# One hybrid decoder block: the memory attention split into three steps that overlap between units, and its second score matmul on all 128 rows

## The chip, the cores and the metric

The kernel runs on one core of a Trainium2 chip. The metric is the time of one execution in device microseconds; lower is better. The engines are TensorE (PE for its matmuls, PEld for its weight loads), VectorE (DVE), ScalarE (ACT), GpSimd (POOL) and SyncE (SP, which here only issues DMAs).

## What is computed

One decoder layer over 1024 tokens of width 1024: a norm, one wide input projection, three mixers (a gated delta rule, a stick-breaking attention, a cross-attention into 256 memory tokens), gates, an output projection and a final norm. The change touches the third mixer alone:

```python
def memory_attention(q, mk, mv):
    s = jnp.einsum('bhtd,bhmd->bhtm', q, mk).astype(jnp.float32) * (1.0 / math.sqrt(q.shape[-1]))
    p = jax.nn.softmax(s, axis=-1)
    return jnp.einsum('bhtm,bhmd->bhtd', p.astype(mv.dtype), mv)
```

There are 4 heads of width 64; q has 1024 rows, mk and mv have 256.

## The kernel before

Operands of matmuls are kept as two parts, high and low (h and l), and a product is three matmuls, high by high, high by low, low by high (helper `mm3`, L160 to L162). The helper `split` makes the parts: ScalarE writes the high part (L143), VectorE the low one (L144).

The input projection is a stream of jobs (`stream`), each of 7 slots of 12 matmuls of 512 columns on TensorE (tiles mmX, mmY, mmZ). Each slot has its weights loaded by SP (L153, tiles wb), subtracted (L203) and split (tiles wu), and its results taken out of PSUM by ScalarE (L230, L247) and VectorE. The PSUM bank of mmZ has one buffer, so a new group of mmZ waits until ScalarE has read the last one at L247.

Beside this stream run generators, which are called between slots in step with the progress of the stream: the triangular solver (VectorE, L648 and L651), then `memory()`, then `combine()` (L717 on: pairs of DMA loads into tiles with one buffer, 64x64 matmuls Y and X, and a store). `memory()` is spread over 32 slots that begin after the job of its queries, `mq`, which stores them to DRAM in parts (mqs_d); these slots belong to the jobs dz and mz.

In `memory()` a unit is one head and 256 rows of q (two blocks of 128). There are 16 units, 4 for each head. The tile q holds a head's high part in rows 0 to 63 and its low part in rows 64 to 127. The tile k holds the high part of k in both halves of its first plane, and the low part in the upper half of its second plane. For each block of a unit the score is two matmuls into the same PSUM tile ms: L683 contracts all 128 rows, L684 contracts 64 rows (high q by low k). Then come the row maximum (L687, L688), the exponential with its sum (L692), the reciprocal (L694), the scaling (L696), four transposes into PSUM tile mT (L700) and a split into pTh and pTl. After two units the value product runs, 6 matmuls into tile mo, and is copied out (L712) and stored (L713). Tiles ms, mo, Y and X share two PSUM banks (tag wk); mT has the tag tr with two.

The program's order is not the order in which the engines run. A planner takes the instructions in the program's order as priorities, simulates them with durations of its own, and writes a fixed list for each engine; so each engine then runs its list in order and waits where something is late.

Of the kernel before, what the change touches and what calls it, by code (L numbers as in the profile page):

```python
# [11 lines left out]
F32 = mybir.dt.float32  # L12
F32R = mybir.dt.float32r
AF = mybir.ActivationFunctionType
ALU = mybir.AluOpType
AX = mybir.AxisListType
# [3 lines left out]
P = 128  # L20
T = 1024
NT = 8
# [15 lines left out]
def hybrid_block(ctx, tc, x, mem, norm_g, mem_norm_g, wq, wv0, wba, convw, a_log, dt_bias,  # L38
                 dn_g, wmk, wmv, wbd, wbs, wbm, wout, final_g, out):
    nc = tc.nc  # L40
    ve, sc, gp, pe, sy = nc.vector, nc.scalar, nc.gpsimd, nc.tensor, nc.sync

    def pool(name, bufs, space=None, side="left", stack=ctx):
        kw = dict(name=name, bufs=bufs, reuse_waits="tile")
        if space is None:
            kw["side"] = side
        else:
            kw["space"] = space
            if space == DRAM:
                kw.pop("reuse_waits")  # L50
        return stack.enter_context(tc.tile_pool(**kw))
# [21 lines left out]
    def psum(tag, name):  # L73
        if tag == "X" and "X" not in banks["tags"]:
            tag = "z"
        if tag in MM:
            return mmp.tile([P, 512], F32, tag=tag, bufs=MM[tag], name=name)
        return banks["pool"].tile([P, 512], F32, tag=tag, bufs=banks["tags"][tag], name=name)
# [4 lines left out]
    ident = cst.tile([P, P], F32, name="ident")  # L83
# [19 lines left out]
    def dscr(name, shape, dt=F32):  # L103
        return dr.tile(shape, dt, name=name)
# [16 lines left out]
    om_d = dscr("om_d", [2, P, T])  # L121
# [3 lines left out]
    mk_d = dscr("mk_d", [2, 2, P, 256])  # L125
    mv_d = dscr("mv_d", [2, P, 2, 256])
    mqs_d = dscr("mqs_d", [2, 4, 64, T])
# [11 lines left out]
    def f(ap):  # L139
        return ap.bitcast(F32)  # L140

    def split(dst, src, on=ve):
        sc.activation(dst[0], src, AF.Copy)  # L143
        on.tensor_tensor(out=dst[1], in0=src, in1=f(dst[0]), op=ALU.subtract)  # L144
# [11 lines left out]
    def mm3(o, pairs, first=True, again=False):  # L156

        n, kw = len(pairs), dict(skip_group_check=True) if again else {}
        for i, (ah, al, bh, bl) in enumerate(pairs):
            pe.matmul(o, ah, bh, start=(first and i == 0), stop=False, **kw)  # L160
            pe.matmul(o, ah, bl, start=False, stop=False, **kw)  # L161
            pe.matmul(o, al, bh, start=False, stop=(i == n - 1), **kw)  # L162
# [89 lines left out]
    def half(i):  # L252
        return slice(i * 512, i * 512 + 512)
# [14 lines left out]
    def row(src, tb):  # L268
        t = ap_.tile([P, T], F32, tag="xt", bufs=4, name=f"xt_{tb}")
        sy.dma_start(out=t, in_=src[0, tb * P:tb * P + P, :])  # L270
        return t
# [92 lines left out]
    rows_ = {tb: row(x, tb) for tb in (0, 4)}  # L364
# [38 lines left out]
    def staged(nm):  # L403
        return st.tile([P, 512], F32, tag="st", bufs=3, name=nm)
# [258 lines left out]
    def memory():  # L663
        mv = [mp_.tile([P, 2, 256], F32R, name=f"mv{j}") for j in "hl"]
        for j in range(2):
            sy.dma_start(out=f(mv[j]), in_=mv_d[j])
        for h in range(4):
            i, r0 = h // 2, (h % 2) * 64

            q = mp_.tile([P, T], F32R, tag="q", bufs=2, name=f"q_{h}")  # L670
            k = mp_.tile([P, 2, 256], F32R, tag="k", bufs=2, name=f"k_{h}")
            for j in range(2):
                sy.dma_start(out=f(q[j * 64:j * 64 + 64]), in_=mqs_d[j, h])
                sy.dma_start(out=f(k[j * 64:j * 64 + 64, 0, :]), in_=mk_d[0, i, r0:r0 + 64])
            sy.dma_start(out=f(k[0:64, 1, :]), in_=mk_d[1, i, r0:r0 + 64])
            for tb in range(0, NT, 2):
                c0 = tb % 4 * P
                if c0 == 0:
                    pT = [mp_.tile([P, 2, 512], F32R, tag=f"pT{j}", name=f"pT{j}_{h}_{tb}") for j in "hl"]
                s = psum("wk", f"ms_{h}_{tb}")  # L680
                for j in range(2):
                    ts = slice((tb + j) * P, (tb + j) * P + P)
                    pe.matmul(s[:, j * 256:(j + 1) * 256], q[:, ts], k[:, 0, :], start=True, stop=False)  # L683
                    pe.matmul(s[:, j * 256:(j + 1) * 256], q[0:64, ts], k[0:64, 1, :], start=False, stop=True)  # L684
                sv = s.rearrange("p (a b) -> p a b", a=2)
                mx = mp_.tile([P, 2], F32, tag="mx", bufs=2, name=f"mx_{h}_{tb}")
                ve.tensor_reduce(out=mx, in_=sv, axis=AX.X, op=ALU.max)  # L687
                ve.tensor_scalar(out=mx, in0=mx, scalar1=-0.125, scalar2=None, op0=ALU.mult)  # L688
                pt = mp_.tile([P, 2, 256], F32, tag="pt", bufs=2, name=f"pt_{h}_{tb}")
                sm = mp_.tile([P, 2], F32, tag="sm", bufs=2, name=f"sm_{h}_{tb}")  # L690
                for j in range(2):
                    sc.activation(pt[:, j, :], sv[:, j, :], AF.Exp, bias=mx[:, j:j + 1], scale=0.125,  # L692
                                  accum_out=sm[:, j:j + 1])
                ve.reciprocal(out=sm, in_=sm)  # L694
                for j in range(2):
                    sc.activation(pt[:, j, :], pt[:, j, :], AF.Copy, scale=sm[:, j:j + 1])  # L696
                o = psum("tr", f"mT_{h}_{tb}")
                for c in range(2):
                    for j in range(2):
                        pe.transpose(o[:, (c * 2 + j) * P:(c * 2 + j + 1) * P], pt[:, j, c * P:(c + 1) * P], ident)  # L700
                split([t[:, :, c0:c0 + 256] for t in pT], o.rearrange("p (a b) -> p a b", a=2))
                yield
                if c0 == 0:
                    continue
                hf = tb // 4
                mo = psum("wk", f"mo_{h}_{hf}")

                hs = slice(i * P, i * P + P)
                mm3(mo, [(mv[0][:, c, hs], mv[1][:, c, hs], pT[0][:, c, :], pT[1][:, c, :])
                                        for c in range(2)])  # L710
                t = staged(f"mot_{h}_{hf}")
                sc.activation(t[r0:r0 + 64], mo[r0:r0 + 64], AF.Copy, scale=0.5)  # L712
                sc.dma_start(out=om_d[i, r0:r0 + 64, half(hf)], in_=t[r0:r0 + 64])  # L713
                yield

    def combine():
# [100 lines left out]
                split([t[:, g * 4:g * 4 + 4, n * P:n * P + P] for t in odn], zt)  # L817
                yield

    SOLVE, MEM, COMB, RECUR = 1 + 1 + 62 + 8, 4 * 6, 16, 1 + 16 * 4  # L820

    def pacer(gen, total):
        done = [0]
# [21 lines left out]
    qk = {}  # L845
# [69 lines left out]
    for c in (15, 13, 11, 9, 7, 5, 3):  # L915
# [5 lines left out]
                            op0=ALU.mult, op1=ALU.mult)  # L921
# [36 lines left out]
    mp_ = pool("M", 1, stack=m_st)  # L958
    while pos[1] <= mark["v"]:
        slot()  # L960
        beside()
    mem_ = pacer(memory(), MEM)
    comb = pacer(combine(), COMB)
    start2 = pos[0]
# [22 lines left out]
    def weights(h, i):  # L987

        w = (i + 1) * P
        t = qk[h]  # L990
        pf = dp.tile([P, T + 1], F32, tag="pf", bufs=2, name=f"pf_{h}_{i}")
        gp.memset(pf[:, T:T + 1], 1.0)  # L992
        off = T - w
        halves = [(0, w)] if w <= 512 else [(w // 2, w), (0, w // 2)]
        ts_ = slice(i * P, i * P + P)
        for c0, c1 in halves:
            o = psum("z", f"z_{h}_{i}_{c0}")[:, 0:c1 - c0]
            mm3(o, [(t["qh"][:, ts_], t["ql"][:, ts_], t["kh"][:, c0:c1], t["kl"][:, c0:c1])])
            be = dp.tile([P, 512], F32, tag="be", bufs=2, name=f"be_{h}_{i}_{c0}")[:, 0:c1 - c0]
            pv = pf[:, off + c0:off + c1]  # L1000
            sc.activation(pv, o, AF.Sigmoid, scale=-SBS)  # L1001
            sc.activation(be, o, AF.Sigmoid, scale=SBS)  # L1002
            if c1 == w:
                for d, fl in ((pf[:, T - P:T], 1.0), (be[:, c1 - c0 - P:c1 - c0], 0.0)):
                    gp.affine_select(out=d, in_=d, compare_op=ALU.is_gt, fill=fl, base=0,  # L1005
                                     pattern=[[-1, P]], channel_multiplier=1)
            ve.tensor_tensor_scan(out=pv[:, ::-1], data0=pv[:, ::-1], data1=pv[:, ::-1],  # L1007
                                  initial=pf[:, off + c1:off + c1 + 1], op0=ALU.mult, op1=ALU.bypass)
            d = pf[:, off + c0 + 1:off + c1 + 1]
            ve.tensor_tensor(out=d, in0=be, in1=d, op=ALU.mult)  # L1010
        return pf[:, off + 1:T + 1]
# [175 lines left out]
    for tb in range(NT):  # L1187
# [11 lines left out]
        for k, hf in order:  # L1199
            s = half(hf)  # L1200
# [5 lines left out]
        for hf in range(2):  # L1206
            s = half(hf)
# [6 lines left out]
        for hf in range(2):  # L1214
            s = half(hf)
# [79 lines left out]
```

## Time and profile before

| | |
|---|---|
| median of 3 runs | 1628.51 us (1625.81 to 1630.97) |
| the profiled execution, own time | 1621.97 us |
| its span, first to last instruction | 1620.3 us |
| TensorE busy | 1549.0 us, 96% |
| VectorE, ScalarE, GpSimd busy | 1180.3, 819.6, 312.5 us |
| mean granted TensorE clock | 0.986 |

The stage in which `memory()` runs lies from about 599 to 782 us of the span. A matmul's duration in the profile is longer than the time it takes up, since matmuls overlap: the distance from one start to the next is what a stream of them costs.

### The profile page before, as it was taken

The page shows a single profiled execution, that of the slowest core. Times are in us where ns is not written, and L with a number is a line of the kernel's source. Part 1 is how long each engine was busy: PE and PEld are TensorE (multiplying, and loading weights), DVE is VectorE, ACT ScalarE, POOL GpSimd, SP SyncE. Part 2 cuts the span into 40 slices and gives each one's busy share as a digit, 9 for nine tenths or more (in the row PEclk, how much of TensorE's full clock was granted, in tenths as well). Part 3 has the DMA queues.
Part 4 walks back from the last instruction along what each step waited for, and adds up shares of the span by engine and source line. Part 5 has one row for each costly group of instructions (what it writes and reads, how often), then busy time and mean ns, then how long its engine had stood idle before and what let it go on. Part 6 is the DMA issues. An engine that isn't in the chain of part 4 may idle for free.

```text
span 1620.3 us, 23277 instructions
## 1 busy us (share of the span) xinstructions
PE 1549.0 (96%) x7979; PEld 1299.1 (80%) x7979; DVE 1180.3 (73%) x1903; ACT 819.6 (51%) x1909; POOL 312.5 (19%) x567
## 2 busy tenths in 40 slices
PE   6899999999999998998999999999998999979998
PEld 6888888887888776776788888888886888868786
DVE  8688989879999997553587778878867755544333
ACT  7578877765555435544455545545554322232121
POOL 4516445331113200000011111111110110110011
PEclk9999999999999998998999999999999999999999
DMA  8337556563333465233322322332138966644232
GB/s 290 97 106 222 160 154 195 164 201 100 109 104 118 143 195 168 83 111 86 119 78 92 103 79 90 107 105 79 66 124 255 304 195 181 206 126 133 82 104 78
DMA packets 152359, 223.32 MB, mean 138 GB/s; under 512 B 39984, under 2 KB 68144, under 8 KB 151984
## 3 DMA queue, kind: packets, MB, share of 16 engines
q1 hardware_dynamic: 107424, 159.94, 32.7%
q10 hardware_dynamic: 35712, 32.51, 6.1%
q0 software_dynamic: 9104, 29.37, 5.4%
q8 instruction: 63, 1.03, 0.3%
q14 instruction: 56, 0.46, 0.1%
HBM read 150.36 MB, written 71.40 MB: 137 GB/s over the span
## 4 chain that ended last, share of the span: by engine, by line
PE 83%; DVE 6%; DMA 5%; ACT 3%; issue 2%; SPq 0%; POOL 0%; ACTq 0%; DVEq 0%; POOLq 0%
PE mmY_g L160 3%; PE mmY_g L162 3%; PE mmY_g L161 3%; PE mmY_skq L160 2%; PE aTp L1033 2%; PE mmY_skq L161 2%; PE mmY_skq L162 2%; PE out L1203 2%; PE out L1201 2%; PE out L1202 2%; PE y_ydn L1135 2%; PE y_ydn L1136 2%; PE y_ydn L1137 2%; PE y_ysb L1136 2%; PE y_ysb L1135 2%
## 5 line engine op out<-in xcount | busy, mean ns | idle before, releaser
L1007 DVE TENSOR_TENSOR_SCAN pf<-pf 128x512 f32<-128x512 f32 (+4 forms) x96 | 97.1, 1012 | 15.7 <-POOL pf L1005 15.7
L143 ACT ACTIVATE aTh<-aTp 128x512 fp32r<-128x512 f32 (+2 forms) x96 | 44.6, 497 | 62.8 <-PE aTp L1033 59.5
L144 DVE TENSOR_TENSOR aTl<-aTp,aTh 128x512 fp32r<-128x512 f32 (+2 forms) x96 | 50.5, 546 | 25.7 <-ACT aTh L143 25.7
L992 POOL MEMSET pf<- 128x1 f32 x64 | 6.0, 98 | 327.0 <-PE aTp L1033 181.0
L1005 POOL TENSOR_SCALAR_AFFINE_SELECT pf<-pf 128x128 f32<-128x128 f32 x64 | 26.5, 415 | 204.7 <-ACT pf L1001 204.7
L1001 ACT ACTIVATE pf<-z 128x512 f32<-128x512 f32 (+4 forms) x96 | 47.1, 498 | 28.6 <-PE z L162 24.9
L1010 DVE TENSOR_TENSOR pf<-be,pf 128x512 f32<-128x512 f32 (+4 forms) x96 | 53.4, 557 | 3.7
L651 DVE TENSOR_TENSOR M<-M,tmp 128x62 f32<-128x62 f32 (+30 forms) x62 | 53.5, 863 | 0.3
L648 DVE TENSOR_TENSOR tmp<-M 128x62 f32<-128x62 f32 (+30 forms) x62 | 53.2, 858 | 0.2
L1201 PE MATMUL out<-oh_wo,mh 128*128 128x512 f32 x128 | 50.0, 391 | 1.5 <-ACT mh L143 1.5
L1135 PE MATMUL y_ydn<-odnh,w_ydn 128*128 128x512 f32 x128 | 49.5, 391 | 1.7 <-ACT odnh L143 1.7
L1049 PE MATMUL av<-aTl,vh 128*128 128x256 f32 (+1 forms) x160 | 47.0, 294 | 3.8 <-DVE aTl L144 3.7
L1135 PE MATMUL y_ysb<-oh_sb,w_ysb 128*128 128x512 f32 x128 | 50.6, 395 | 0.0
L1137 PE MATMUL y_ysb<-oh_sb,w_ysb 128*128 128x512 f32 x128 | 50.5, 395 | 0.0
L1136 PE MATMUL y_ysb<-ol_sb,w_ysb 128*128 128x512 f32 x128 | 50.3, 393 | 0.0
L1137 PE MATMUL y_ydn<-odnh,w_ydn 128*128 128x512 f32 x128 | 49.9, 390 | 0.0
L1136 PE MATMUL y_ydn<-odnl,w_ydn 128*128 128x512 f32 x128 | 49.8, 389 | 0.0
L1202 PE MATMUL out<-ol_wo,mh 128*128 128x512 f32 x128 | 49.8, 389 | 0.0
L1002 ACT ACTIVATE be<-z 128x512 f32<-128x512 f32 (+4 forms) x96 | 47.3, 503 | 4.2 <-DVE pf L1010 4.0
L1203 PE MATMUL out<-oh_wo,ml 128*128 128x512 f32 x128 | 49.3, 389 | 0.0
L1048 PE MATMUL av<-aTh,vh 128*128 128x256 f32 (+1 forms) x160 | 45.2, 283 | 1.4 <-ACT aTh L143 1.4
L1208 DVE TENSOR_TENSOR xo<-out,xo 128x512 f32<-128x512 f32 x16 | 11.0, 691 | 48.0 <-PE out L1203 48.0
(818 smaller groups left out, 5535.4 us busy)
## 6 DMA issues: line engine op xcount, KB each, us to landing
wb_g_b<-in_wq_dram SPq DMA_DIRECT2D x48, 256.0 KB, 2.8
wb_kq_b<-in_wq_dram SPq DMA_DIRECT2D x32, 256.0 KB, 3.0
wb_skq_b<-in_wq_dram SPq DMA_DIRECT2D x32, 256.0 KB, 2.7
g_d<-g ACTq DMA_DIRECT2D x32, 256.0 KB, 2.0
xt<-in_x_dram SPq DMA_DIRECT2D x8, 512.0 KB, 4.6
wb_sz_b<-in_wq_dram SPq DMA_DIRECT2D x16, 256.0 KB, 3.6
kt_d<-kq ACTq DMA_DIRECT2D x16, 256.0 KB, 3.4
gam<-gr_d SPq DMA_DIRECT2D x8, 512.0 KB, 4.4
```

What stands on the lines that cost most here:

```text
L160: pe.matmul(o, ah, bh, start=(first and i == 0), stop=False, **kw)
L161: pe.matmul(o, ah, bl, start=False, stop=False, **kw)
L162: pe.matmul(o, al, bh, start=False, stop=(i == n - 1), **kw)
L651: ve.tensor_tensor(out=d, in0=d, in1=t, op=ALU.add)
L1007: ve.tensor_tensor_scan(out=pv[:, ::-1], data0=pv[:, ::-1], data1=pv[:, ::-1], initial=pf[:, off + c1:off + c1 + 1], op0=ALU.mult, op1=ALU ...
L1010: ve.tensor_tensor(out=d, in0=be, in1=d, op=ALU.mult)
L1135: pe.matmul(oo[hf], wh, oh[:, s], start=(k == 0), stop=False)
L1136: pe.matmul(oo[hf], wh, ol[:, s], start=False, stop=False)
L1137: pe.matmul(oo[hf], wl, oh[:, s], start=False, stop=(k == n - 1))
L1201: pe.matmul(oo[hf], mh[:, k, :], wo[k][0][:, s], start=(k == 0), stop=False)
L1202: pe.matmul(oo[hf], mh[:, k, :], wo[k][1][:, s], start=False, stop=False)
L1203: pe.matmul(oo[hf], ml[:, k, :], wo[k][0][:, s], start=False, stop=(k == KC - 1))
```

## The change

The loop over heads and blocks is cut into four functions. `operands(h)` loads q and k of a head; `scores(n)` does unit n up to its scaled weights; `weights(n)` does its transposes and split; `values(p)` does the value product of units 2p and 2p+1 and its store. They are issued so that `scores(n)` stands ahead of `weights(n-1)` and `values(p)` stands behind `scores(2p+3)`; operands of the next head are issued at the second unit of a head. The k tile now holds the high part of k in both halves of the first plane and the low part in both halves of the second, so that both score matmuls contract 128 rows (high and low q by high k, high and low q by low k). A head's k is loaded with two DMAs of both planes in place of three of one plane. The number of steps over which the pacing spreads the generator goes from 24 to 40, over the same 32 slots.

```diff
-            for j in range(2):
-                sy.dma_start(out=f(q[j * 64:j * 64 + 64]), in_=mqs_d[j, h])
-                sy.dma_start(out=f(k[j * 64:j * 64 + 64, 0, :]), in_=mk_d[0, i, r0:r0 + 64])
-            sy.dma_start(out=f(k[0:64, 1, :]), in_=mk_d[1, i, r0:r0 + 64])
...
-                    pe.matmul(s[:, j * 256:(j + 1) * 256], q[:, ts], k[:, 0, :], start=True, stop=False)
-                    pe.matmul(s[:, j * 256:(j + 1) * 256], q[0:64, ts], k[0:64, 1, :], start=False, stop=True)
...
+            for j in range(2):
+                rows_ = slice(j * 64, j * 64 + 64)
+                sy.dma_start(out=f(q[rows_]), in_=mqs_d[j, h])
+                sy.dma_start(out=f(k[rows_]), in_=mk_d[:, i, r0:r0 + 64].rearrange("j d m -> d j m"))
+            qk[h] = q, k
+
+        def scores(n):
+            h, tb = units[n]
+            q, k = qk[h]
+            s = psum("wk", f"ms_{h}_{tb}")
+            for j in range(2):
+                for c in range(2):
+                    pe.matmul(s[:, j * 256:(j + 1) * 256], q[:, (tb + j) * P:(tb + j) * P + P], k[:, c, :],
+                              start=(c == 0), stop=(c == 1))
...
+        operands(0)
+        for n in range(18):
+            if n % 4 == 1 and n < 13:
+                operands(n // 4 + 1)
+            if n < 16:
+                scores(n)
                 yield
...
+            if n % 2 and n > 2:
+                values((n - 3) // 2)
+                yield
+            if 1 <= n <= 16:
+                weights(n - 1)
                 yield
...
-    SOLVE, MEM, COMB, RECUR = 1 + 1 + 62 + 8, 4 * 6, 16, 1 + 16 * 4
+    SOLVE, MEM, COMB, RECUR = 1 + 1 + 62 + 8, 40, 16, 1 + 16 * 4
```

The other instructions of a unit (maximum, exponential, scaling, transposes, split, value product) are the same as before, in number and shape, and so are the tiles' buffer counts.

## Rows read from the trace of the kernel before

**Rows 1.** The page: span, busy time of TensorE, and the chain that ended last by engine.

```profile
span 1620.3 us, 23277 instructions
...
PE 1549.0 (96%) x7979; PEld 1299.1 (80%) x7979; DVE 1180.3 (73%) x1903; ACT 819.6 (51%) x1909; POOL 312.5 (19%) x567
...
PE 83%; DVE 6%; DMA 5%; ACT 3%; issue 2%; SPq 0%; POOL 0%; ACTq 0%; DVEq 0%; POOLq 0%
```

**Rows 2.** Busy time by stretch, the whole stage first, then parts of it. Columns: stretch in us, its length, then busy us (and instructions) of PE, PEld, DVE, ACT and POOL, then the granted TensorE clock as a share of full speed, the DMA share and GB/s.

```profile
598.90:782.00 183.10, 167.21 (x853) 126.57 (x854) 103.57 (x189) 88.52 (x199) 1.10 (x3) 0.93 0.41 118
```

**Rows 3.** The same view, parts of the stage.

```profile
612.50:617.00 4.50, 0.18 (x1) 0.00 (x0) 2.78 (x7) 4.25 (x12) 0.00 (x0) 0.87 0.13 50
617.00:626.40 9.40, 8.68 (x22) 5.35 (x22) 8.10 (x20) 4.46 (x11) 0.91 (x1) 0.52 0.07 28
626.40:664.00 37.60, 36.84 (x162) 28.34 (x162) 23.86 (x44) 22.33 (x53) 0.00 (x0) 1.00 0.60 183
...
733.00:736.50 3.50, 0.29 (x4) 0.09 (x2) 1.85 (x5) 2.52 (x7) 0.00 (x0) 0.83 0.90 219
736.50:745.00 8.50, 7.81 (x42) 6.32 (x43) 1.98 (x3) 1.19 (x2) 0.00 (x0) 0.50 0.08 19
...
762.00:774.00 12.00, 9.22 (x56) 6.83 (x57) 4.16 (x7) 4.39 (x9) 0.20 (x2) 0.86 0.29 71
```

**Rows 4.** The instructions on tile ms (scores): durations in ns, least, median and most, and the first and last start.

```profile
L683 PE MATMUL ms<-k,q x32: 276/384/581, 607.3 to 758.2; 128*128 128x256 f32 x32
...
L684 PE MATMUL ms<-k,q x32: 379/382/579, 607.5 to 758.6; 64*128 64x256 f32 x32
```

**Rows 5.** TensorE in order of time around the first two units' scores: start and busy time in us. The 8 score matmuls run from 607.26, and the next matmul is a dense one at 609.65.

```profile
607.26 0.28 PE L683 MATMUL ms<-k,q 128*128 128x256 f32 x1
607.46 0.38 PE L684 MATMUL ms<-k,q 64*128 64x256 f32 x1
...
609.65 0.50 PE L160 MATMUL mmY_dz<-hS3h,wu_dz_T 128*128 128x512 f32 x1
609.98 0.39 PE L161 MATMUL mmY_dz<-hS3l,wu_dz_T 128*128 128x512 f32 x1
610.21 0.40 PE L162 MATMUL mmY_dz<-hS3h,wu_dz_T 128*128 128x512 f32 x1
```

**Rows 6.** TensorE in order of time in an earlier stage, where matmuls of 256 columns that all contract 128 rows follow each other, each with a weight load of its own (13 of them from 37.57 to 39.00).

```profile
37.57 0.28 PE L161 MATMUL mv<-wu_mv,hS4h 128*128 128x256 f32 x1
...
39.00 0.28 PE L161 MATMUL mv<-wu_mv,hS4h 128*128 128x256 f32 x1
```

**Rows 7.** Groups of TensorE instructions from 598 to 782 us by line and shape: busy us, mean ns of one, and TensorE's idle time just before them with what ended it.

```profile
L683 PE MATMUL ms<-k,q 128*128 128x256 f32 x32 | 12.2, 382 | 1.4 <-ACT mot L712 1.4
L700 PE MATMUL mT<-ident,pt 128*128 128x128 f32 x64 | 12.1, 307 | 4.4 <-ACT pt L696 4.4
L726 PE MATMUL Y<-tmpc 64*64 64x64 f32 x128 | 10.1, 233 | 4.1 <-DMA tmpc<-mo_d 3.2 <-ACT wu_skq_T L143 0.9
...
L160 PE MATMUL mo<-pTh,mvh 128*128 128x512 f32 x16 | 8.2, 514 | 3.6 <-ACT pTh L143 3.5
```

**Rows 8.** TensorE in order of time, pieces of the stage; in brackets the idle time before the instruction and what ended it.

```profile
617.04 2.15 PE L700 MATMUL mT<-ident,pt 128*128 128x128 f32 x8 [4.36 <-ACT pt L696]
619.88 0.79 PE L160 MATMUL mo<-pTh,mvh 128*128 128x512 f32 x1 [0.69 <-ACT pTh L143]
...
626.44 0.50 PE L160 MATMUL mmZ_dz<-hS4h,wu_dz_B 128*128 128x512 f32 x1
...
679.91 0.79 PE L726 MATMUL Y<-tmpc 64*64 64x64 f32 x10
...
736.48 1.94 PE L726 MATMUL Y<-tmpc 64*64 64x64 f32 x16 [3.21 <-DMA tmpc<-mo_d]
...
743.36 0.63 PE L162 MATMUL mo<-pTh,mvl 128*128 128x512 f32 x1
743.78 0.63 PE L160 MATMUL mo<-pTh,mvh 128*128 128x512 f32 x1
...
765.18 0.50 PE L160 MATMUL mo<-pTh,mvh 128*128 128x512 f32 x1 [0.69 <-ACT pTh L143]
...
780.40 1.14 PE L732 MATMUL X<-tmpc,T1c 64*64 64x64 f32 x16
```

**Rows 9.** ScalarE in order of time in the same stretch as the first two lines of the group before; in brackets its idle time and what ended it.

```profile
612.72 0.63 ACT L143 ACTIVATE wu_dz_T<-wt_dz_T 128x512 fp32r<-128x512 f32 x1 [4.14 <-PE mmY_dz L162]
613.36 1.28 ACT L692 ACT_TABLE_LOAD   x1
...
624.88 0.59 ACT L712 ACTIVATE mot<-mo 64x512 f32<-64x512 f32 x1 [0.33 <-PE mo L162]
625.37 0.58 ACT L247 ACTIVATE dz<-mmZ_dz 128x512 f32<-128x512 f32 x1
```

**Rows 10.** DMA issues from 585 to 782 us: what, how many, KB each, median us from issue to landing.

```profile
tmpc<-mo_d SPq DMA_DIRECT2D x8, 128.0 KB, 3.6
k<-mk_d SPq DMA_DIRECT2D x12, 64.0 KB, 3.9
```

**Rows 11.** Waits of SP's DMA queue from 580 to 775 us: line, whom it waited for, us in total, times, longest.

```profile
SPq L721 <- PE X L732: 30.4, 7, 7.1
...
SPq L673 <- PE ms L684: 8.2, 1, 8.2
```

More of the change, by code (lines that the diff above doesn't have):

```diff
@@ L666, in memory, with operands @@
             sy.dma_start(out=f(mv[j]), in_=mv_d[j])
-        for h in range(4):
+        units = [(h, tb) for h in range(4) for tb in range(0, NT, 2)]
+        qk, pts, pTs = {}, {}, {}
+        def operands(h):
             i, r0 = h // 2, (h % 2) * 64
@@ L672, in memory @@
             for j in range(2):
-                sy.dma_start(out=f(q[j * 64:j * 64 + 64]), in_=mqs_d[j, h])
-                sy.dma_start(out=f(k[j * 64:j * 64 + 64, 0, :]), in_=mk_d[0, i, r0:r0 + 64])
-            sy.dma_start(out=f(k[0:64, 1, :]), in_=mk_d[1, i, r0:r0 + 64])
[L676 to L680, printed above, removed]
-                for j in range(2):
-                    ts = slice((tb + j) * P, (tb + j) * P + P)
-                    pe.matmul(s[:, j * 256:(j + 1) * 256], q[:, ts], k[:, 0, :], start=True, stop=False)
-                    pe.matmul(s[:, j * 256:(j + 1) * 256], q[0:64, ts], k[0:64, 1, :], start=False, stop=True)
[L685 to L690, printed above, removed]
-                for j in range(2):
[L692 to L701, printed above, removed]
-                yield
[L703 to L713, printed above, removed]
@@ new lines, in operands @@
+                rows_ = slice(j * 64, j * 64 + 64)
[10 more added lines that the diff above has]
+                              start=(c == 0), stop=(c == 1))
+            sv = s.rearrange("p (a b) -> p a b", a=2)
+            mx = mp_.tile([P, 2], F32, tag="mx", bufs=2, name=f"mx_{h}_{tb}")
+            ve.tensor_reduce(out=mx, in_=sv, axis=AX.X, op=ALU.max)
+            ve.tensor_scalar(out=mx, in0=mx, scalar1=-0.125, scalar2=None, op0=ALU.mult)
+            pt = mp_.tile([P, 2, 256], F32, tag="pt", bufs=2, name=f"pt_{h}_{tb}")
+            sm = mp_.tile([P, 2], F32, tag="sm", bufs=2, name=f"sm_{h}_{tb}")
+            for j in range(2):
+                sc.activation(pt[:, j, :], sv[:, j, :], AF.Exp, bias=mx[:, j:j + 1], scale=0.125,
+                              accum_out=sm[:, j:j + 1])
+            ve.reciprocal(out=sm, in_=sm)
+            for j in range(2):
+                sc.activation(pt[:, j, :], pt[:, j, :], AF.Copy, scale=sm[:, j:j + 1])
+            pts[n] = pt
@@ new lines, in weights @@
+        def weights(n):
+            h, tb = units[n]
+            pt = pts.pop(n)
+            if n % 2 == 0:
+                pTs[n // 2] = [mp_.tile([P, 2, 512], F32R, tag=f"pT{j}", name=f"pT{j}_{n}") for j in "hl"]
+            c0 = n % 2 * 256
+            o = psum("tr", f"mT_{h}_{tb}")
+            for c in range(2):
+                for j in range(2):
+                    pe.transpose(o[:, (c * 2 + j) * P:(c * 2 + j + 1) * P], pt[:, j, c * P:(c + 1) * P], ident)
+            split([t[:, :, c0:c0 + 256] for t in pTs[n // 2]], o.rearrange("p (a b) -> p a b", a=2))
@@ new lines, in values @@
+        def values(p):
+            h, hf = p // 2, p % 2
+            i, r0 = h // 2, (h % 2) * 64
+            pT = pTs.pop(p)
+            mo = psum("wk", f"mo_{h}_{hf}")
+            hs = slice(i * P, i * P + P)
+            mm3(mo, [(mv[0][:, c, hs], mv[1][:, c, hs], pT[0][:, c, :], pT[1][:, c, :]) for c in range(2)])
+            t = staged(f"mot_{h}_{hf}")
+            sc.activation(t[r0:r0 + 64], mo[r0:r0 + 64], AF.Copy, scale=0.5)
+            sc.dma_start(out=om_d[i, r0:r0 + 64, half(hf)], in_=t[r0:r0 + 64])
```

## The prediction

> **What bounds the kernel now.** I read the page first. TensorE is busy for 1549.0 of 1620.3 us, and the chain that ended last is TensorE for 83% [rows 1]: whatever TensorE saves shortens the kernel, as long as its next work is ready. But busy time alone doesn't show a slow matmul from a fast one, so I went to the stage that the change touches, from 598.9 to 782 us. There TensorE is busy 167.2 of 183.1 us, at a granted clock of 0.93, beside VectorE at 103.6 and ScalarE at 88.5 [rows 2]. So TensorE bounds this stage too; the other two have room on average, and can only hurt by what they do late. TensorE loses time here in three ways, and each needs a view of its own: idle time (the groups by line, then the list in order of time), stretches at half clock (the table by stretch), and instructions that cost more than their columns (distances from start to start).
>
> **The score matmuls.** This is the largest term. A score matmul has 256 columns, and the median durations of both forms, 384 and 382 ns, are near each other [rows 4]. What counts is the distance of starts: the eight of the first two units run from 607.46 (the second) to 609.65 (the dense matmul behind the eighth), 7 steps in 2.19 us or 0.313 us each [rows 5]. Elsewhere, matmuls of 256 columns that all contract 128 rows run from 37.57 to 39.00 in 12 steps, 0.119 us each, with a weight load each as here [rows 6]. The reader should see in rows 5 that the first one, which follows a dense matmul of 128 rows, has the short duration (0.28 us), and that only from the switch between 128 and 64 rows on each is 0.38: the alternation is what costs, as though nothing of the next could start before the last had left the array. After the change all 64 contract 128 rows. So 64 x (0.313 - 0.119) = 12.4 us fall away. The borders of a group nearly cancel: the first score matmul took 0.20, less than 0.313, and the dense one behind the group took 0.33 (609.65 to 609.98) in place of 0.23 (609.98 to 610.21) [rows 5]. Bounds: at best 0.313 goes to 0.119 for all, 12.4; at worst the new pairs, which load the same q twice, keep 0.313 and it is 0. I take 12.4, since rows 6 are the same shape with a load each.
>
> The Trainium skill bears on this in two places that disagree. TensorE: Matmul & The Clock Gate (section "Why this matters for your kernels") says that a single matmul that contracts few rows takes the same time as a full one; by that alone filling the rows would bring nothing, and the sum would lack 12.4. TensorEngine Tiling (Array Packing) (section "Tiling Modes") says that a change of tiling mode drains the engine; by that the alternation is the cost. The rows (0.28 us before the first switch, 0.38 after) speak for the second.
>
> **The idle time of the memory's own chain.** Within the stage TensorE idles 4.4 us before transposes (waiting for the scaled weights), 3.6 before the value product (waiting for the high part of the split) and 1.4 before scores (waiting for a PSUM bank that L712 reads) [rows 7]. The 3.6 and 1.4 are seven gaps of about 0.7 us, as at 619.88 and 765.18 [rows 8]: transposes, split and value product stand right behind one another. In the new order the value product stands behind the scores of another unit and more than a slot of dense matmuls (40 steps over 32 slots); a slot is 12 matmuls at 0.23 us, 2.8 us, and hides them. Only the last head, where the pipeline runs empty, still has its transposes, split and value product in a row, so I keep two gaps: 5.0 - 1.4 = 3.6 us fall away (bounds 0 and 5.0). The 4.4 us gap is one: at 617.04 eight transposes wait for the softmax of the first units [rows 8]. ScalarE stood at a weight conversion until 612.72, loaded a table for 1.28 us, and only then did the exponentials [rows 9]. In the new order the scores of the next unit and steps of the stream are ahead of these transposes. I take it as gone, 4.4 us; it is the most doubtful part, since the first scores start at 607.3 [rows 4], 8 us into the stage, when several steps of `memory()` are overdue at once, so that the planner may still put them close together (bound: 0).
>
> **The half clock.** Behind this gap, from 617.0 to 626.4, the granted clock is 0.52, the lower of the two levels, 1.2 GHz, with TensorE busy 8.68 us [rows 3]. At 2.4 GHz such work takes about half, so some 4.3 us hang on the gap before it; they go if the gap goes. A second stretch, 736.5 to 745.0 at 0.50, follows an idle stretch of 3.2 us that a load of `combine()` ended [rows 3, 8]; there value matmuls start 0.42 us apart (743.36 to 743.78). Half of its 7.81 us busy, 3.9 us, is lost, and the change has no hand in that load: I keep it. A third, 762 to 774 at 0.86, loses 0.14 x 12 = 1.7 us; kept as well.
>
> **Things at nothing.** The k loads: 12 of 64 KB become 8 of 128 KB; loads of 128 KB in this stage land in 3.6 us, those of k in 3.9 [rows 10], and they are issued a unit or more ahead. If they came late, the scores of a head would wait up to that, four times, at most 15.6 us; what hides them is a head's remaining three units. On SP, L673 waited once for 8.2 us for the last scores of an earlier head [rows 11], with the weight loads of the stream queued behind it. That wait stays: the third head's loads need the first head's tiles. New waits: the exponential of unit n+1 needs the tile of weights of unit n-1 to be transposed (two buffers); behind it on ScalarE wait weight conversions and evacuations of the stream. The transposes stand ahead of those scores on TensorE, so I cost it at nothing; if TensorE is late there, it costs ScalarE up to a slot, 2.8 us. The matmuls of scores, transposes and values keep their number.
>
> **Sum.** 12.4 + 3.6 + 4.4 + 4.3 = 24.7 us off the profiled execution, 1621.97 to 1597.3. That execution lies 6.5 us under the median of the runs, so on the runs' scale it is 1628.5 - 24.7 = 1603.8, taken as 1604.
>
> **The rivals.**
>
> The first gap stays. Late queries make a pile of steps, ScalarE still has to load its table and do the exponentials, and the transposes wait as before; then the half clock behind it stays too. Left: 12.4 + 3.6 = 16.0 us, 1612.5. For it: ScalarE's order in rows 9. Against: two further slots of dense work now stand ahead of the transposes.
>
> Everything goes: with fewer waits the later half clocks vanish too. 12.4 + 5.0 + 4.4 + 9.9 = 31.7 us, 1597. Against: the 3.2 us wait for `combine()`'s load [rows 7].
>
> `combine()` sets the end of the stage. Its loads wait for its last matmuls, 30.4 us over 7 waits [rows 11], and its eight heads run from 679.9 to 781.5 [rows 8]. If that pace doesn't change, what is saved behind 679.9 becomes idle time. By the share of the stage that lies there, 102 of 183 us, that is 0.56 of the 12.4 and the 3.6, 9.0 us. Left: 24.7 - 9.0 = 15.7 us, 1612.8. Against: eight loads of 3.6 us [rows 10] and these waits make 59 of its 101.6 us, so it has slack.
>
> The change doesn't do what it says on TensorE: equal matmuls with the same weights loaded twice still run 0.313 apart. The first page cited above would have it so. Left: 12.3 us, 1616; with the first gap standing too, 3.6 us, 1625.
>
> Slower: ScalarE serves the memory ahead of the stream. In the profile the dense matmuls ended before 612.7 and the next mmZ started at 626.44, because ScalarE read that bank (L247) at 625.37 only, behind the memory's exponentials, splits and L712 [rows 8, 9]. In those 13.8 us the memory's matmuls would take some 5.0 us at full clock (8 transposes half of the 2.15 shown at half clock, 8 scores at 0.313, 6 value matmuls at 0.23), so one such block costs 8.8 us. With two units open at a time, ScalarE has more memory work that the planner ranks ahead. If it happened once for each head, three blocks more, 26.4 us are lost against 16.0 gained: 10.4 us slower, 1638.9. It decides from the second additional block on (16.0 / 8.8 = 1.8). Against: from 626.4 to 664 the same mix ran at full clock with 36.84 of 37.60 us busy [rows 3].
>
> **How the numbers follow.** Forecast 0.38; first gap stays 0.25; everything goes 0.14; `combine()` 0.10; scores not faster 0.07; slower 0.06. A measurement of this kernel can tell about 0.3% (4.9 us) from no change. Faster by more: all but the slower case, half of the case of slow scores and some slack in the rest, 0.88. Within: 0.07. Slower: 0.05. The range reaches from 1592, a few us past the case in which everything goes (small switches around the score groups that I let cancel could add), to 1617, past the first-gap, `combine()` and slow-score cases; some 0.2 is left out.
>
> **What would show it.** Right: in the profile after, score matmuls start about 0.12 us apart with durations near 0.28; no gap of 4 us before transposes and no half clock right behind the first units; nearly no idle time ended by the split before value matmuls; the stage shorter by 20 us or more, and the stages behind it unchanged in length. Wrong: score steps near 0.3 us; a first gap of the old size; new idle time before mmZ with L247 as its end, or before Y with a load as its end; a later stage that grew, since the planner lays out its lists anew.

## The result and the profile after

The changed kernel takes 1609.66 us (median of 6 runs, 1605.6 to 1612.86) beside 1628.64 of the kernel before: ratio 0.9882, 95% interval 0.9862 to 0.9903, so 19 us faster, where 24.7 were forecast. A second measurement (below) gives 0.9896. The profiled execution took 1605.6 us with a span of 1603.9, 16.4 us less than that of the kernel before. It is the fastest of the six, with the highest mean clock (0.991; the others had 0.984 to 0.988), so a second profile of the same kernel stands beside it below. Two executions among the experiments, of 3452 us (kernel before) and 3937 us (the order alone with loads ahead), were in a slow state and are left out of the ratios.

The scores, tile ms, of the kernel after (durations in ns: least, median, most; all 64 now have one form):

```profile
L687 PE MATMUL ms<-k,q x64: 274/282/580, 608.5 to 732.4; 128*128 128x256 f32 x64
```

The median was 384 and 382 [rows 4]. TensorE in order of time, pieces of the stage:

```profile
608.45 1.19 PE L687 MATMUL ms<-k,q 128*128 128x256 f32 x8
609.48 0.40 PE L162 MATMUL mmY_dz<-hS2h,wu_dz_T 128*128 128x512 f32 x1
...
614.49 1.11 PE L687 MATMUL ms<-k,q 128*128 128x256 f32 x8
615.45 0.75 PE L712 MATMUL mT<-ident,pt 128*128 128x128 f32 x4
616.56 0.33 PE L712 MATMUL mT<-ident,pt 128*128 128x128 f32 x1 [0.37 <-ACT pt L700]
...
621.96 0.49 PE L160 MATMUL mo<-pTh,mvh 128*128 128x512 f32 x1 [1.79 <-ACT pTh L143]
...
729.73 1.93 PE L752 MATMUL Y<-tmpc 64*64 64x64 f32 x16 [3.38 <-DMA tmpc<-mo_d]
...
733.53 0.63 PE L162 MATMUL mo<-pTh,mvl 128*128 128x512 f32 x1
733.95 0.63 PE L160 MATMUL mo<-pTh,mvh 128*128 128x512 f32 x1
```

From the first of eight score matmuls to the matmul behind them it is 1.03 us (608.45 to 609.48); it was 2.39 before (607.26 to 609.65) [rows 5]. Where TensorE stood for 4.4 us before the first transposes [rows 8], it now runs the scores of two further units and dense matmuls, and waits 0.37. But the wait for a load of `combine()` is there as before, 3.38 us, and behind it value matmuls start 0.42 us apart again: half clock. The table by stretch (columns as in rows 2), whole stage and parts:

```profile
598.90:764.00 165.10, 151.48 (x868) 122.14 (x869) 104.41 (x194) 87.73 (x203) 1.15 (x3) 0.98 0.47 135
...
612.00:617.00 5.00, 4.63 (x26) 3.67 (x25) 4.01 (x11) 4.99 (x16) 0.00 (x0) 1.00 0.24 60
617.00:626.00 9.00, 6.79 (x37) 5.39 (x38) 8.72 (x24) 6.04 (x18) 0.00 (x0) 1.00 0.50 142
...
720.00:740.00 20.00, 15.02 (x94) 12.01 (x94) 7.99 (x16) 8.49 (x21) 0.00 (x0) 0.83 0.31 78
```

The stage is 18 us shorter (183.1 in [rows 2]). The clock is 1.00 from 612 to 626 in this execution, where it was 0.52 behind the first gap [rows 3]. What is left of half clock stands at 720 to 740. Groups of TensorE with the idle time before them (columns as in rows 7):

```profile
L687 PE MATMUL ms<-k,q 128*128 128x256 f32 x64 | 11.2, 304 | 0.5 <-ACT pt L696 0.4
L712 PE MATMUL mT<-ident,pt 128*128 128x128 f32 x64 | 10.4, 278 | 1.5 <-ACT pt L700 1.4
L752 PE MATMUL Y<-tmpc 64*64 64x64 f32 x128 | 10.1, 233 | 5.5 <-DMA tmpc<-mo_d 5.5
L758 PE MATMUL X<-tmpc,T1c 64*64 64x64 f32 x128 | 9.1, 221 | 1.1 <-ACT pt L696 1.1
L160 PE MATMUL mo<-pTh,mvh 128*128 128x512 f32 x16 | 7.1, 446 | 1.9 <-ACT pTh L143 1.8
```

The memory's own idle time fell from 9.4 us (4.4 + 3.6 + 1.4 [rows 7]) to 3.9; that before the matmuls of `combine()` rose from 4.1 to 6.6. Of these 6.6 us, 5.5 before Y end with a load. The 1.1 before X end with the memory's exponential (L696 in this kernel), which reads the scores out of one of the two PSUM banks that X shares.

### The profile page after: what moved, and what is told of

Its sections match the earlier page's. It is cut to its first block, busy times and chain, and to the rows that moved or that the text cites. A ratio compares the mean times of both kernels' runs of the same rounds, so it can differ in the third digit from the quotient of the medians.

```text
span 1603.9 us, 23268 instructions
## 1 busy us (share of the span) xinstructions
PE 1532.3 (96%) x7979; PEld 1292.5 (81%) x7979; DVE 1179.0 (74%) x1903; ACT 817.3 (51%) x1909; POOL 315.4 (20%) x567
## 3 DMA queue, kind: packets, MB, share of 16 engines
q8 instruction: 63, 1.03, 0.3%
## 4 chain that ended last, share of the span: by engine, by line
PE 62%; DMA 5%; DVE 4%; issue 4%; ACT 2%; POOL 1%; SPq 0%; POOLq 0%; DVEq 0%; ACTq 0%
PE mmY_g L160 3%; PE mmY_g L162 3%; PE mmY_g L161 3%; PE mmY_skq L160 2%; PE mmY_skq L162 2%; PE mmY_skq L161 2%; PE out L1229 2%; PE out L1227 2%; PE out L1228 2%; PE y_ydn L1161 2%; PE y_ydn L1162 2%; PE y_ydn L1163 2%; PE aTp L1059 2%; PE y_ysb L1161 2%; PE y_ysb L1163 2%
## 5 line engine op out<-in xcount | busy, mean ns | idle before, releaser
L1033 DVE TENSOR_TENSOR_SCAN pf<-pf 128x512 f32<-128x512 f32 (+4 forms) x96 | 97.2, 1013 | 15.7 <-POOL pf L1031 15.6
```

## The experiments

**The changed kernel once more.** 

> The changed kernel once more, to see what belongs to one execution: the stage of the memory again 18 us shorter, ratio 0.988. Where the stages behind the stick-breaking attention are longer than before by 3 us again, the planner's new lists cost that; where they are not, it was that one execution.

Measured: 1607.87 us, ratio 0.9896 (0.9877 to 0.9916). The stretch from the first branch matmul y_ym to the first `out` matmul, by the table by stretch: before, after, and this execution.

```profile
1235.30:1524.70 289.40, 275.02 (x1522) 237.13 (x1521) 154.93 (x309) 78.57 (x228) 24.76 (x48) 0.99 0.60 185
```

```profile
1216.00:1508.60 292.60, 277.73 (x1522) 238.39 (x1520) 153.02 (x305) 77.65 (x226) 24.72 (x48) 0.99 0.58 180
```

```profile
1218.10:1510.70 292.60, 278.59 (x1522) 240.16 (x1521) 152.95 (x305) 77.35 (x226) 24.59 (x48) 0.98 0.58 180
```

The changed kernel loses 3.2 us there in both executions, which speaks for its lists and against one execution's chance. Nothing in that stretch was edited. In the other kernels of this study the same stretch takes 288.2 to 293.8 us, one execution each.

The second execution differs in one thing that matters. Behind the same gap of 1.79 us before the first value product, where the first execution kept its clock, this one fell to half clock; value matmuls then start 0.42 us apart:

```profile
622.61 0.50 PE L160 MATMUL mo<-pTh,mvh 128*128 128x512 f32 x1 [1.79 <-ACT pTh L143]
...
624.75 0.63 PE L160 MATMUL mo<-pTh,mvh 128*128 128x512 f32 x1
625.17 0.63 PE L161 MATMUL mo<-pTl,mvh 128*128 128x512 f32 x1
```

```profile
618.00:627.00 9.00, 6.80 (x29) 5.21 (x29) 8.67 (x26) 5.67 (x17) 0.00 (x0) 0.85 0.53 138
...
598.00:690.00 92.00, 88.05 (x459) 71.36 (x457) 69.44 (x136) 56.91 (x137) 0.93 (x1) 0.98 0.56 161
690.00:790.00 100.00, 91.85 (x519) 73.59 (x520) 49.55 (x81) 44.67 (x90) 1.07 (x4) 0.95 0.38 109
```

So the half clock that one profile shows is known to some microseconds only.

**Each part alone.** The first edit is to the kernel before, the second to the changed one:

```diff
-                sy.dma_start(out=f(k[j * 64:j * 64 + 64, 0, :]), in_=mk_d[0, i, r0:r0 + 64])
-            sy.dma_start(out=f(k[0:64, 1, :]), in_=mk_d[1, i, r0:r0 + 64])
+                sy.dma_start(out=f(k[j * 64:j * 64 + 64]), in_=mk_d[:, i, r0:r0 + 64].rearrange("j d m -> d j m"))
...
-                    pe.matmul(s[:, j * 256:(j + 1) * 256], q[0:64, ts], k[0:64, 1, :], start=False, stop=True)
+                    pe.matmul(s[:, j * 256:(j + 1) * 256], q[:, ts], k[:, 1, :], start=False, stop=True)
```

```diff
-                sy.dma_start(out=f(k[rows_]), in_=mk_d[:, i, r0:r0 + 64].rearrange("j d m -> d j m"))
+                sy.dma_start(out=f(k[rows_, 0, :]), in_=mk_d[0, i, r0:r0 + 64])
+            sy.dma_start(out=f(k[0:64, 1, :]), in_=mk_d[1, i, r0:r0 + 64])
...
-                for c in range(2):
-                    pe.matmul(s[:, j * 256:(j + 1) * 256], q[:, (tb + j) * P:(tb + j) * P + P], k[:, c, :],
-                              start=(c == 0), stop=(c == 1))
+                ts = slice((tb + j) * P, (tb + j) * P + P)
+                pe.matmul(s[:, j * 256:(j + 1) * 256], q[:, ts], k[:, 0, :], start=True, stop=False)
+                pe.matmul(s[:, j * 256:(j + 1) * 256], q[0:64, ts], k[0:64, 1, :], start=False, stop=True)
```

> The kernel before with one part of the change: k stored twice and both score matmuls on 128 rows; the order of units as before. My theory: the alternation of 128 and 64 rows cost 0.19 us at each of 64 score matmuls, and TensorE is what the stage waits for, so 11 to 13 us fall away by this alone (ratio near 0.993); score matmuls start 0.12 us apart; the gap of 4.4 us before the first transposes and the half clock behind it stay. Rival A: the order is what pays, and faster score matmuls only lengthen the waits for the softmax that follows them: under 5 us. Rival B: the idle time and the half clock go with it, since the planner lays out its lists anew: over 17 us.

> The changed kernel with its second score matmul put back on 64 rows (k loaded as before): the new order alone. My theory: the memory's own idle time (5.6 us) and the half clock behind the first gap go, the score matmuls stay 0.31 us apart: 5 to 8 us faster than before (ratio near 0.996), so that the two parts add up to the 19 of the whole. Rival A: the order brings most of it, 13 us or more. Rival B: nothing or slower, since the new order moves waits to the loads of the combine step.

Measured: 128-row scores alone 0.9944 (0.9929 to 0.996), 9.1 us; the order alone 0.9986 (0.9974 to 0.9998), 2.3 us. Both are under my numbers, and their sum, 11.4, is well under the whole, 17 to 19: the parts need each other. For the order, the rival that its waits move to the loads of the combine step came nearest in the time of the whole kernel. But the profiled executions put much of that shortfall elsewhere. From the first dz matmul of the stage to the first y_ym the order alone takes 630.5 us where the kernel before took 636.4: 5.9 us less, as my theory had it. It loses 2.1 us ahead of that stretch and 4.3 behind it, in stages that no edit touches (before: 289.40, above):

```profile
1231.50:1525.20 293.70, 278.56 (x1521) 239.74 (x1520) 153.52 (x305) 78.00 (x226) 23.97 (x48) 0.98 0.57 179
```

By the same measure the scores alone win 5.4 us and the whole 18.4 to 19.9, so the parts need each other within the stage too. Where the half clock stands, by stretch; the scores alone, then the order alone (the column before the last two is the clock):

```profile
598.00:690.00 92.00, 82.97 (x388) 66.06 (x389) 64.32 (x121) 51.48 (x119) 0.91 (x1) 0.93 0.51 147
690.00:790.00 100.00, 89.70 (x520) 71.15 (x518) 44.99 (x78) 40.84 (x88) 0.20 (x2) 0.88 0.38 108
```

```profile
598.00:690.00 92.00, 88.50 (x404) 68.12 (x403) 66.21 (x129) 52.72 (x125) 0.92 (x1) 0.98 0.51 154
690.00:790.00 100.00, 92.78 (x521) 71.96 (x520) 44.84 (x75) 40.21 (x86) 0.20 (x2) 0.91 0.37 106
```

Length times what the clock lacks to 1.00 gives the loss to the half clock (a little too much, since idle time is in it): 6.4 + 12.0 = 18.4 us with the scores alone, 1.8 + 9.0 = 10.8 with the order alone, 0.07 x 183.1 = 12.8 before [rows 2], 0.02 x 165.1 = 3.3 after, and 1.8 + 5.0 = 6.8 in the second execution after. So the scores alone won their 11 us of matmul time and lost a part of it to more half clock; the order alone took most of the first stretch away and kept the second, behind 690, where `combine()` runs. From this I formed the theory that the waits for the loads of `combine()` hold the rest.

**Is it the switch of rows?** Both are edits to the kernel before. In the first the scores are not the full sums of their two products; the second leaves out one product.

```diff
-                for j in range(2):
-                    ts = slice((tb + j) * P, (tb + j) * P + P)
-                    pe.matmul(s[:, j * 256:(j + 1) * 256], q[:, ts], k[:, 0, :], start=True, stop=False)
-                    pe.matmul(s[:, j * 256:(j + 1) * 256], q[0:64, ts], k[0:64, 1, :], start=False, stop=True)
+                for c in range(2):
+                    for j in range(2):
+                        ts = slice((tb + j) * P, (tb + j) * P + P)
+                        r_ = slice(0, (P, 64)[c])
+                        pe.matmul(s[:, j * 256:(j + 1) * 256], q[r_, ts], k[r_, c, :], start=(c == 0), stop=(c == 1),
+                                  skip_group_check=True)
```

```diff
-                    pe.matmul(s[:, j * 256:(j + 1) * 256], q[:, ts], k[:, 0, :], start=True, stop=False)
+                    pe.matmul(s[:, j * 256:(j + 1) * 256], q[0:64, ts], k[0:64, 0, :], start=True, stop=False)
```

> The kernel before with the four score matmuls of a unit in another order: both of 128 rows, then both of 64, so two switches in a unit in place of four; the same matmuls otherwise. Theory of the switch: two of four steps fall from 0.313 to 0.12 us, 32 x 0.19 = 6 us faster. Rival: a matmul of 64 rows is itself slow, or loading the same weights twice in a row is: no change within 1.5 us, the steps stay at 0.31 by form.

> The kernel before with both score matmuls on 64 rows; it leaves out the product of the low part of q with the high part of k. Theory of the switch: no switch within a group of scores, steps near 0.12 us, so nearly the gain of the 128-row scores, 7 to 11 us. Rival: 64 rows are slow as such, steps of 0.31 us, within 2 us of before.

Measured: half as many switches 0.9972 (0.9959 to 0.9985), 4.6 us; all on 64 rows 0.9921 (0.9901 to 0.9941), 12.8 us, above my 7 to 11 (8.1 us by the profiled executions, up to y_ym). TensorE in order of time, first with half the switches, then with 64 rows only:

```profile
609.73 1.69 PE L685 MATMUL ms<-k,q 128*128 128x256 f32 x8
611.34 0.50 PE L160 MATMUL mmY_dz<-hS3h,wu_dz_T 128*128 128x512 f32 x1
```

```profile
605.92 0.38 PE L683 MATMUL ms<-k,q 64*128 64x256 f32 x1
606.14 0.28 PE L684 MATMUL ms<-k,q 64*128 64x256 f32 x1
606.26 0.28 PE L683 MATMUL ms<-k,q 64*128 64x256 f32 x1
606.38 0.28 PE L684 MATMUL ms<-k,q 64*128 64x256 f32 x1
606.59 0.50 PE L162 MATMUL mmY_dz<-hS2h,wu_dz_T 128*128 128x512 f32 x1
606.92 0.40 PE L160 MATMUL mmY_dz<-hS2h,wu_dz_T 128*128 128x512 f32 x1
```

Eight scores take 1.61 us with half the switches (2.39 before, 0.95 for eight steps of 0.119). Matmuls of 64 rows follow each other at 0.12 us like those of 128; only the first (0.22) and the ones around the return to 128 rows (0.21 and 0.33) pay. So the switch is the cost, and not the 64 rows, nor q as weights loaded twice in a row, which the 64-row kernel does as well.

**The loads of the combine step ahead.** The loads of consecutive heads get four places in the solver's matrix M, which is dead by then, in place of one tile. The tile of Y and X, in the line of `u`, goes from one buffer to two with it; no run separates the two. The edit is added to the kernel before, to either part alone, and to the changed kernel.

```diff
-        M = vp.tile([P, 64, 64], F32, name="M")
+        M = slv["M"] = vp.tile([P, 64, 64], F32, name="M")
...
-            t, u = (vp.tile([P, 2, 512], F32, tag=n, name=f"{n}c_{h}") for n in ("tmp", "T1"))
+            m = slice(h % 4 * 16, h % 4 * 16 + 16)
+            t = slv["M"][:, m, :].rearrange("p a b -> p (a b)").rearrange("p (a b) -> p a b", a=2)
+            u = vp.tile([P, 2, 512], F32, tag=("tmp", "T1")[h % 2], name=f"uc_{h}")
```

> The kernel before with the combine step's loads ahead in the same way, nothing of the change: the control. Theory: its 3.2 us wait for the load and most of the half clock behind it go, 5 to 8 us faster than before (ratio near 0.996). Rival: within 2 us of before, since the idle time moves to the next wait.

> The kernel with the 128-row scores alone (9 us faster than before), with the loads of the combine step given four places in the solver's matrix, which is dead by then, in place of one tile, so that they are issued well ahead. My theory, formed on the last runs: the two parts of the change together save more than their sum (19 against 9 and 2) because each part alone leaves or adds half-clock stretches of TensorE behind the combine step's load waits (in the profile of the 128-row scores alone, 0.5 to 0.55 in 730 to 740 and 760 to 770). Without those waits the scores alone should come to 16 to 20 us under the kernel before. Rival: the half clock comes from thin work beside the softmax waits, whatever the loads do: no more than 3 us beyond the 9.

> The new order of the units with the second score matmul on 64 rows (2 us faster than before) and the combine step's loads ahead: the last corner of the eight combinations of scores, order and loads. My theory: behind the loads' waits lay what the order alone could not give; the idle time before Y and the half clock near 745 of that kernel go, so 14 to 19 us faster than before, and the three parts then add up (128-row scores 11 to 15 us whatever the other two are, once nothing waits). Rival: the loads help only where TensorE's own work is short; then this stays at 2 + 5 = 7 us.

> The changed kernel with the combine step's loads ahead. Theory: what the change left, 5.5 us of waits before Y and a half clock of some 3 us at 730, goes: 6 to 9 us faster than the changed kernel, ratio near 0.984 to the kernel before. Rival: no change within 2 us against the changed kernel.

Measured, as gain in us over the kernel before, worked out as (1 - ratio) x 1625.5 (near the medians of the kernel before beside these runs, 1625.2 to 1625.9); each gain is known to some 2 to 3.5 us:

| | loads as before | loads ahead |
|---|---|---|
| kernel before | 0 | 5.4 (0.9967, 0.995 to 0.9983) |
| 128-row scores alone | 9.1 | 17.9 (0.989, 0.9872 to 0.9908) |
| order alone | 2.3 | 23.7 (0.9854, 0.9837 to 0.987) |
| both, the change | 16.9 and 19.2 | 33.8 (0.9792, 0.9774 to 0.9811) |

The control and the scores came as expected; the other two gained more than I expected (23.7 against 14 to 19; 15 to 17 over the changed kernel against 6 to 9). With the loads ahead the two parts nearly add up: 17.9 + 23.7 - 5.4 = 36.2 against 33.8. By stretch, the loads ahead alone, the order with loads ahead, the change with loads ahead:

```profile
598.00:690.00 92.00, 83.74 (x351) 62.39 (x350) 62.10 (x117) 48.72 (x113) 0.92 (x1) 0.93 0.56 154
690.00:790.00 100.00, 96.94 (x565) 75.20 (x564) 50.72 (x87) 46.64 (x99) 0.20 (x2) 0.97 0.37 103
```

```profile
598.00:690.00 92.00, 88.37 (x411) 67.96 (x410) 66.60 (x130) 52.77 (x125) 0.92 (x1) 0.98 0.62 166
690.00:790.00 100.00, 99.29 (x583) 79.77 (x583) 54.66 (x89) 50.17 (x102) 1.70 (x4) 1.00 0.37 106
```

```profile
598.00:690.00 92.00, 87.14 (x476) 71.01 (x475) 69.35 (x135) 57.37 (x137) 0.96 (x1) 1.00 0.65 172
690.00:790.00 100.00, 98.50 (x572) 80.73 (x571) 61.14 (x97) 52.41 (x105) 3.87 (x9) 1.00 0.36 103
```

The half clock loses 0.07 x 92 + 0.03 x 100 = 9.4 us with the loads alone, 1.8 with the order and the loads, and nothing with all three. So the second stretch needs the loads and the first the order, and 128-row scores are worth 9.1 us by themselves, 15 to 17 on the order, 12.5 on the loads and 10.1 on both. The groups of the last kernel:

```profile
L754 PE MATMUL Y<-M 64*64 64x64 f32 x128 | 9.3, 221 | 0.0
L760 PE MATMUL X<-M,uc 64*64 64x64 f32 x128 | 9.1, 221 | 0.9 <-ACT pt L696 0.9
```

The wait before Y is gone, that before X is not. The first and last starts of Y and X (after the durations in ns), in the changed kernel and in the same kernel with loads ahead:

```profile
L752 PE MATMUL Y<-tmpc x128: 218/218/333, 664.7 to 758.8; 64*64 64x64 f32 x128
L758 PE MATMUL X<-tmpc,T1c x128: 218/218/267, 673.1 to 762.8; 64*64 64x64 f32 x128
```

```profile
L754 PE MATMUL Y<-M x128: 218/218/267, 664.5 to 739.1; 64*64 64x64 f32 x128
L760 PE MATMUL X<-M,uc x128: 218/218/267, 670.7 to 743.5; 64*64 64x64 f32 x128
```

The eight heads of `combine()` ran over 101.6 us before (679.9 to 781.5 [rows 8]), over 98.3 in the changed kernel and over 79.3 with the loads ahead (with 228 and 207 dense matmuls among them).

Not all of this is the stage. The last stretch, from y_ym to `out`, is 4.0 us shorter here than in the changed kernel:

```profile
1200.40:1489.00 288.60, 274.74 (x1522) 237.08 (x1521) 155.02 (x309) 78.53 (x228) 24.74 (x48) 0.99 0.60 185
```

Between the first dz matmul and y_ym this kernel takes 603.1 us where the changed one took 616.5, so some 13 us of its gain lie there; its profiled execution is the fastest of its five. Differences of some 3 us in the table above can lie in lists of other stages.

At 1592.03 us (median of 5 runs) it is the fastest kernel of this study, ahead of both given ones.

**The combine step earlier.** `CF = 0.85` becomes `CF = 0.80` in the changed kernel.

> The changed kernel with the combine step begun earlier in the stream (at 0.80 of its progress in place of 0.85, so over 23 slots in place of 17), its loads as in the changed kernel. Theory: its heads stand further apart, so the waits before Y and the half clock behind them shrink without any new buffer: 3 to 8 us faster than the changed kernel (ratio to before 0.984 to 0.987). Rival: the planner packs the heads as tightly as its own load durations allow, so the waits stay: within 2 us of the changed kernel.

Measured: 0.9879 (0.9858 to 0.99), 19.7 us, the changed kernel's own gain. Neither account holds whole: the time is the rival's, but the loads' waits went, and others took their place, with half clock behind them (0.66 from 680 to 690, behind the 2.9 us before Y).

```profile
L752 PE MATMUL Y<-tmpc 64*64 64x64 f32 x128 | 9.9, 233 | 3.1 <-ACT pTh L143 2.9 <-DMA tmpc<-mo_d 0.2
```

```profile
680.00:690.00 10.00, 9.03 (x41) 7.66 (x42) 4.90 (x10) 4.68 (x12) 0.00 (x0) 0.66 0.13 41
```

## Why the prediction was right, and by how much it was off

The forecast was right in its direction, and 1609.66 lies in the range; it lies nearer to the `combine()` rival (1612.8) than to the likeliest case (1604), and the terms show why. Term by term, against the two profiled executions (starts added up from the lists in order of time, from the first dz matmul to the first y_ym):

| | forecast | measured |
|---|---|---|
| score matmuls | 12.4 | 11.3 (20.45 to 9.19) |
| the memory's idle time | 8.0 | 5.5 (9.4 to 3.9) |
| half clock, seen in the dense, value, X, Y and transpose matmuls | 4.3 | 7.5 |
| waits of `combine()` | 0 | -2.5 (4.1 to 6.6) |
| other idle time up to y_ym | 0 | -2.1 |
| from y_ym to `out` | 0 | -3.2 |
| sum | 24.7 | 16.5, of 16.4 |

In the second execution of the changed kernel the half clock gives 4.9 in place of 7.5 and the other idle time -0.2 in place of -2.1; the rest agrees within 0.6. That the half clock came out above my 4.3 is no merit of the sum: it holds parts of the second and third stretch, which I had kept.

**Scores.** The term was right, and the half-switch and the 64-row kernels show its cause. About 1 us of its 11.3 was half clock: eight of the scores before ran behind the first gap (1.80 and 1.87 us for four, 1.15 at full clock), four of those after behind the load wait (1.01, 0.57 at full clock). The drain at a change of mode, as the Trainium skill has it in TensorEngine Tiling (Array Packing), section "Tiling Modes", agrees with the trace: (2.39 - 0.95) / 8 = 0.18 us for each of these matmuls. And the sentence of the Trainium skill in TensorE: Matmul & The Clock Gate, section "Why this matters for your kernels", that a single matmul of few contracted rows takes as long as a full one agrees too, as long as none of another form stands between (0.12 us either way). I had set the two against each other, and they hold side by side.

**The first gap** went for the reason given: the scores of two further units and dense matmuls run in its place. The half clock behind it went in the first execution and shrank to 1.8 us in the second. The case that it stays, to which I gave 0.25, did not come. What I mis-sized is the small gaps: I let all but two of seven go, but 1.79 us before the first value product is one new wait of their kind. That its steps are overdue together there, as I feared for the transposes, is argued and not shown.

**The step that failed** is the one on `combine()`, where I kept its load wait and its half clock as they were. The wait for a load before Y grew (3.2 to 5.5 us), and the half clock behind it remained. That it grew because less work of TensorE lies between one head and the next load is argued; the scores alone, which shorten that work most simply, raise it to 5.8. I had this as a rival at 0.10, with a fixed pace as its mechanism, and that was too little: the eight heads take 98.3 us where they took 101.6 (13 dense and 5 value matmuls more stand among them, some 4 us of work). The other 15.7 us of the stage's saving lie ahead of the first Y, where the same 204 dense and 40 score matmuls take 65.3 us in place of 81.0. With the loads ahead the heads take 79.3 us, and some 13 us hung on these waits (and on the second buffer that came with that edit), as much as the largest term of my sum. I also sized the half clock from one execution, and it moves by some 3 us between two executions of one kernel. Why each part alone has more of it behind 690 than both together, with the loads as before, stays open.

**Given back later.** The 3.2 us behind y_ym stand in two executions of the changed kernel. That they come from the planner's new lists is argued from this alone; no run isolates which instruction does it. Of the signs that I had named for being wrong, two showed: idle time before Y with a load as its end, and a later stage that grew. The stage itself is 18 us shorter, where I had asked for 20.

**Slower.** ScalarE holds up dense matmuls through L247 three times (1.45, 0.29 and 0.45 us), 2.2 us in all and no more than before (2.5), far from the three further blocks that this case needed. My reading of the one block before was wrong as well: the mmZ matmul at 626.44 follows the last score matmul there without idle time [rows 8], so the 8.8 us that I put on L247 were the first gap and its half clock over again (4.4 + 4.3).

## What to carry to other kernels

Where matmuls that contract all rows alternate with ones that contract half, look at the distance of starts: filling the rows with data that is there anyway can pay for every switch. When a stage loses to several waits, a part tested alone can look worthless (the order: 2.3 us in all, 5.9 up to y_ym); test it with the neighbouring wait removed (23.7 against 5.4, so 18.3 us), and look at where in the span the time went. A list laid out anew moves time in stages that were not edited, here some 3 us.

## What the hardware showed unexpectedly

The matmuls of 64 rows are as quick as those of 128 among themselves (0.12 us for 256 columns); each switch costs about 0.2 us. The clock went to 1.2 GHz behind gaps of 4.36 us in the kernel before and of 3.38 in the changed one. Behind a gap of 1.79 us it went either way: in one execution of the changed kernel it stayed at 2.4 GHz (granted clock 1.00 from 617 to 626, TensorE busy 6.79 of 9.00 us), in the other it fell (0.85 from 618 to 627, busy 6.80 of 9.00), with the same list of instructions. So the length of a gap alone does not tell, in these traces, whether the clock falls.
